# An encoder layer in split-float32 matmuls: a written-out step sequence for every weight block, 121 seven-product pairs for 116, joined weight sums, and q/k/v scaling moved to ScalarE

## The chip, the cores and the metric

The kernel runs on one core of one Trainium2 chip. The metric is the device time of one execution in microseconds (us); the median of the runs counts. The engines are TensorE (PE; its weight loads are listed as PEld), VectorE (DVE), ScalarE (ACT), GpSimd (POOL) and SyncE (SP, which issues the loads).

## The reference, cut to what matters

One encoder layer on 256 tokens of width 4096, all in float32. Nearly all the work is in the large matrix products:

```python
h = rms_norm(x, g_mix[i])
proj = einsum('bsd,de->bse', h, w_in[i])          # 4096 x (1024+512+64 + 5*2048)
c_q, c_kv, k_rope, gate_a, q_b, k_b, v_b, gate_b = split(proj, ...)
... # latent attention (16 heads) from c_q, c_kv, k_rope through w_uq, w_ukv
... # dilated attention (16 heads) from q_b, k_b, v_b
y_a = rms_norm(y_a, g_out_mla[i]) * silu(gate_a)
y_b = rms_norm(y_b, g_out_dil[i]) * silu(gate_b)
x = x + einsum('bse,ed->bsd', concatenate([y_a, y_b]), w_out[i])      # 4096 x 4096
ple = einsum('bsc,cd->bsd', p[i], w_ple[i])
gate = sigmoid(einsum('bsd,de->bse', rms_norm(x, g_ple[i]), w_ple_gate[i]))  # 4096 x 4096
x = x + ple * gate
return rms_norm(x, g_final)
```

## The kernel before, in words

**One product is three matmuls.** Float32 operands are split in two parts, `hi` (a rounded copy, made by ScalarE) and `lo` (the rest, made by VectorE as `src - hi`); `mm` adds hi x hi, hi x lo and lo x hi into one bank of PSUM. So each 512 KB row block of weights that arrives in a buffer `raw` costs a conversion: 1024 columns on ScalarE and 1024 on VectorE.

**Blocks.** The large products are cut into 18 blocks of 1024 weight columns (`Block`): six for the dilated q, k and v (called D0 to D5 here), five for the latent query and the gates (G0 to G4), three for `w_out` (O0 to O2) and four for `w_ple_gate` (P0 to P3). Each block goes over 32 rows of 128 weights (k-rows), with two token tiles A1 and A2 and two column halves of 512, so that there are four results. A block has two kinds of steps:

- A *plain* step (`plain_step`, `c` in an order string) takes one k-row: four products, 12 matmuls.
- A *fast pair* (`fast_steps`, four `f` in an order string) takes two k-rows at once by the seven products of Strassen's method in Winograd's form. Its four steps issue M1; M2 and M3; M5 and M7; M6 and M4: seven products, 21 matmuls, where two plain steps have 24. For them VectorE makes four sums of weights (512 columns each), which are then split into hi and lo as well. The sums of activations that a pair needs are made once for all the blocks that share them (`add_sums`: `x_sums` for D, `x_sums2` for G, `y_sums` for O, `x1_sums` for P).

The seven products add up in eight banks: M1, M5, M6 and M7 belong to the fast pairs, M2, X, M3 and M4 to both kinds. After the last fast step of a block a task called *mid* (`d_mid`, `gate_mid`, `out_mid`, `wide_mid`) combines M1, M5, M6 and M7 in SBUF, while the block's trailing plain steps run; the next block's M2, X, M3 and M4 use the banks that mid reads. After the last step a task *done* adds the other four banks. In the D blocks and in G0 mid and done also multiply each token by its normalisation factor `rx`, as the scalar operand of VectorE's instructions.

**The order of steps.** `spread(n, lead, trail)` makes a block's sequence from three numbers: a lead of plain steps, n pairs and the rest of the plain steps mixed by a fixed cost balance, and a trail of plain steps. `FAST_QKV`, `FAST_G`, `FAST_O` and `FAST_P` give the pairs of each block: 3 7 8 8 8 7, 3 6 7 7 7, 6 7 6 and 7 7 7 5, 116 in all.

**The order of the work around them.** Every engine runs its instructions in the order in which the program issues them. The program keeps a planning clock (`Clock`) with a cost for each instruction, converts the weights a few steps ahead of PE (`convert`, `lead` is `AHEAD` = 2 steps, and 3 more where a block has further places for converted weights), and runs the tasks (mid, done, sums, transposes, attention heads) in the gaps that this clock sees (`advance`). Loads are issued by SP into four `raw` buffers in turn; a pair needs two of them at once.

**Gates and heads.** An attention head's output is copied from PSUM by ScalarE (`attend`), later multiplied by the gate and by the gain of the branch's norm in `gate_rest`, one head (256 columns) at a time.

Of the kernel before, what the change touches and what calls it, by code (L numbers as in the profile page):

```python
# [12 lines left out]
F32 = mybir.dt.float32  # L13
# [21 lines left out]
WARM = 6, 3  # L35

# [174 lines left out]
def encoder_layer(ctx: ExitStack, tc: tile.TileContext, x, p, positions, g_mix, w_in, g_q_latent, w_uq,  # L211
# [30 lines left out]
    def plain(t):  # L242
        return t.bitcast(F32)

# [344 lines left out]
    def attend(h, q_src, k_src, pe, v, y, dil):  # L589
# [96 lines left out]
        nc.scalar.activation(y, by_token(o) if dil else o, AF.Copy)  # L686
# [16 lines left out]
    def head_unit(name, load, product, tags, done, n=2, time=48 * 0.119):  # L703
# [3 lines left out]
        def step(j):  # L707
            box = []

            def get():  # L710
                box.append(clock.made(wp.tile([P, 2, Q], F32, tag="raw", name=f"raw_{name}_{j}", bufs=RAW), "raw", RAW))
                load(box[0], j)
# [11 lines left out]
            new.ring, new.ring_id = HEADS_RING, "heads"  # L724
# [104 lines left out]
    def turn_steps(n, tags):  # L829
# [4 lines left out]
        def step(j):  # L834
            box = []

            def load():
                box.append(clock.made(wp.tile([P, 2, Q], F32, tag="raw", name=f"raw_r{n}_{j}", bufs=RAW), "raw", RAW))
# [19 lines left out]
            new.ring, new.ring_id = HEADS_RING, "heads"  # L858
# [53 lines left out]
    def gate_rest(dil, c, u):  # L912
# [6 lines left out]
        for b in range(2):  # L919
# [17 lines left out]
    QUARTERS = (0, 0, "M2"), (1, 1, "X"), (0, 1, "M3"), (1, 0, "M4")  # L937

    def gate_mid(tags, blk, after=()):

        def task():
# [9 lines left out]
            for d, a, b in (((1, 1), (0, 0), "M6"), ((1, 0), (1, 1), "M5"), ((0, 1), (1, 1), "M7"),  # L951
                            ((1, 1), (0, 1), "M5")):
                nc.vector.tensor_tensor(e[d[0]][:, d[1]], e[a[0]][:, a[1]], ps[b], op=ALU.add)
# [58 lines left out]
    def d_mid(key, blk):  # L1012
        def task():
# [11 lines left out]
            yield from awaited("rx")  # L1025
            sc = [(rxq if key[0] == "q" else rx)[:, t:t + 1] for t in range(NT)]

            def add(h, t, m, old):
                nc.vector.scalar_tensor_tensor(d[h][:, t], ps[m], sc[t], old, op0=ALU.mult, op1=ALU.add)
# [12 lines left out]
    def d_done(key, blk):  # L1042
        def task():
# [3 lines left out]
            for m, t, h in quarters[2:] + quarters[:2] if key == ("v", 1) else quarters:  # L1047
                nc.vector.scalar_tensor_tensor(d[h][:, t], blk.ps[m], sc[t], d[h][:, t], op0=ALU.mult, op1=ALU.add)
# [88 lines left out]
    class Step:  # L1137

        banks, holds, ahead = (), (), False
# [4 lines left out]
        def __init__(self, load, split, run, needs=(), frees=0, time=2.73):  # L1144
            self.load, self.split, self.run, self.needs, self.frees, self.after = load, split, run, needs, frees, None
            self.hold, self.mid = 0, False
# [5 lines left out]
    class Block:  # L1152
# [19 lines left out]
        def step(self, which, *args):  # L1172
            new = Step(*args)
            new.n = self.q
# [12 lines left out]
        def load(self, kt):  # L1187
            kt = self.row(kt)
            r = clock.made(wp.tile([P, 2, self.q], F32, tag="raw", name=f"raw_{kt}", bufs=RAW), "raw", RAW)
# [4 lines left out]
        def plain_step(self, kt):  # L1194
            box, first_ = [], self.late and kt == 16
# [17 lines left out]
            return [self.step("M2 X M3 M4", lambda: box.append(self.load(kt)), both, run, self.needs(kt), 1)]  # L1213

        def fast_steps(self, j):

            r, T = [], []
# [4 lines left out]
            def sub(dst, a, b):  # L1222
                nc.vector.tensor_tensor(dst, a, b, op=ALU.subtract)

            def split1(hi, lo):
                if isinstance(self.tmp, tuple):
                    T.extend(slot(b, [2, self.q]) for b in self.tmp)
                else:
                    both = slot(self.tmp, [4, self.q])
                    T.extend((both[:, :2], both[:, 2:]))  # L1230
                sub(T[0][:, 0], r[0][:, 1], r[0][:, 0])
                sub(T[0][:, 1], r[0][:, 1], r[1][:, 1])
                split(hi[:, 0], lo[:, 0], r[0][:, 0])

            def split2(hi, lo):
                nc.scalar.activation(hi, r[1], AF.Copy)
                sub(T[1][:, 0], r[1][:, 1], T[0][:, 0])
                sub(T[1][:, 1], r[1][:, 0], T[1][:, 0])
                nc.vector.tensor_tensor(lo, r[1], plain(hi), op=ALU.subtract)

            def run(*which):
                def go(hi, lo):
                    for i, (m, a) in enumerate(which):
# [5 lines left out]
            return [  # L1249
                self.step("M1", tuple(lambda k=k: r.append(self.load(k)) for k in (2 * j, 2 * j + 1)), split1, run(("M1", A11)), needs, 1, 0.69),  # L1250
                self.step("M2 M3", None, split2, run(("M2", A12), ("M3", S(3))), needs, 1, 1.37),
                self.step("M5 M7", None, lambda hi, lo: split(hi, lo, T[0]), run(("M5", S(0)), ("M7", S(2))), more, 0, 1.37),
                self.step("M6 M4", None, lambda hi, lo: split(hi, lo, T[1]), run(("M6", S(1)), ("M4", A22)), more, 0, 1.37),
            ]

    def add_sums(n, pair, dst, tmp, name, out, free=lambda j: True, first=0):
# [3 lines left out]
        def task():  # L1260
# [10 lines left out]
            for j in range(first, n):  # L1271
# [806 lines left out]
```

## Time and profile before

| what | value |
|---|---|
| runs of the kernel | 1898.52, 1899.08, 1900.08 us |
| median | 1899.08 us |
| profiled execution, span from first to last instruction | 1897.4 us |
| the same beside the median of the runs | 1.7 us less (its own device time is not listed apart) |
| busy: PE / PEld / DVE / ACT | 1878.5 / 1579.8 / 1696.8 / 1140.2 us |
| weights and other loads | 364.72 MB read, 194 GB/s over the span |

The busy time of an engine is the union of its instructions' durations. The durations of matmuls overlap, so that the time from the start of one to the start of the next is the measure, and a busy PE can still have small gaps; a stretch without gaps is seen in the sum of the weight loads, since each matmul has one of about the same length. An instruction's row has its start, its duration, the engine, the kernel's line (here always that of a helper), the operation, what it writes and reads by the program's names, and its shape.

### The profile page before, as it was taken

Reading aid. Unit: us, or ns where it says so; the run is one execution under the profiler, and the core shown is the slowest. Engines: PE = TensorE matmul, PEld = TensorE weight load, DVE = VectorE, ACT = ScalarE, POOL = GpSimd, SP = SyncE. Lnnn points to the kernel's source line nnn. Section 1 sums busy time; section 2 is a strip of 40 time slices with the busy share of each in tenths; the row PEclk is TensorE's granted clock in tenths of the full one; section 3 lists DMA queues with packets and bytes.
Section 4 is the critical chain, followed back from the end, with each engine's and each line's share of the span. In section 5 each row is a group of like instructions: output and inputs, shape, how many; then the busy total and the mean of one; then the engine's idle time right before and its main releaser. Section 6 shows DMA issues by size and latency. Waiting matters only on the chain.

```text
span 1897.4 us, 25417 instructions
## 1 busy us (share of the span) xinstructions
PE 1878.5 (99%) x9133; PEld 1579.8 (83%) x9133; DVE 1696.8 (89%) x2354; ACT 1140.2 (60%) x1543; POOL 31.2 (2%) x41
## 2 busy tenths in 40 slices
PE   9999999999999999999999999999999999999997
PEld 7888888888899888888888999888888888888885
DVE  6999999899898989999998777999989989989897
ACT  7655656565588555556556556656655555666654
POOL 0000000000011000000000010100000000000000
PEclk9999999999999999999999999999999999999999
DMA  8666666666735566666667553576666666665665
GB/s 279 189 205 213 214 212 200 198 213 193 218 84 159 166 211 183 196 215 189 208 199 209 137 142 123 167 231 204 216 199 217 187 194 218 194 223 183 221 222 180
DMA packets 160871, 370.59 MB, mean 195 GB/s; under 512 B 29116, under 2 KB 70952, under 8 KB 160744
## 3 DMA queue, kind: packets, MB, share of 16 engines
q1 hardware_dynamic: 159896, 366.58, 62.0%
q0 software_dynamic: 512, 1.84, 0.3%
q8 instruction: 72, 1.18, 0.3%
q10 hardware_dynamic: 336, 0.54, 0.1%
q14 instruction: 55, 0.45, 0.1%
HBM read 364.72 MB, written 4.19 MB: 194 GB/s over the span
## 4 chain that ended last, share of the span: by engine, by line
PE 85%; DVE 10%; DMA 2%; issue 2%; ACT 1%; POOL 0%; DVEq 0%; ACTq 0%; POOLq 0%
PE m L177 49%; PE t L177 16%; PE s L177 11%; PE o L177 9%; DVE lo L177 3%; DVE B L177 3%; DVE T L177 2%; DVE Ah L177 1%; DMA raw<-in_w_ple_gate_dram 1%; DVE Al L177 1%; DMA raw<-in_w_in_dram 1%; ACT hi L177 0%; DVE st L177 0%; ACT B L177 0%; DVE B7b L177 0%
## 5 line engine op out<-in xcount | busy, mean ns | idle before, releaser
L177 ACT ACTIVATE hi<-raw 128x1024 fp32r<-128x1024 f32 (+2 forms) x396 | 378.9, 966 | 278.1 <-PE m L177 70.9
L177 DVE TENSOR_TENSOR lo<-raw,hi 128x1024 fp32r<-128x1024 f32 (+2 forms) x396 | 433.4, 1107 | 61.8 <-ACT hi L177 60.6
L177 PE MATMUL m<-hi,Ah 128*128 128x512 f32 (+2 forms) x659 | 247.2, 387 | 0.3 <-ACT hi L177 0.3
L177 DVE TENSOR_TENSOR B<-raw,B 128x1024 fp32r<-128x1024 f32 (+3 forms) x228 | 213.9, 947 | 20.5 <-ACT B L177 18.8
L177 PE MATMUL m<-hi,Al 128*128 128x512 f32 (+2 forms) x625 | 229.6, 380 | 0.0
L177 PE MATMUL m<-lo,Ah 128*128 128x512 f32 (+2 forms) x549 | 207.8, 379 | 1.4 <-DVE lo L177 1.3
L177 ACT ACTIVATE B<-raw 128x1024 fp32r<-128x1024 f32 (+2 forms) x142 | 135.3, 962 | 96.8 <-DMA raw<-in_w_in_dram 25.3
L177 PE MATMUL m<-hi,B 128*128 128x512 f32 (+1 forms) x524 | 179.0, 389 | 0.0
L177 PE MATMUL m<-B,Ah 128*128 128x512 f32 (+2 forms) x554 | 146.7, 359 | 0.6 <-DVE B7b L177 0.6
L177 PEld LDWEIGHTS m<-hi,Ah 128*128 128x128 f32 x659 | 124.0, 188 | 22.7 <-ACT hi L177 1.2
L177 PEld LDWEIGHTS m<-hi,Al 128*128 128x128 f32 x625 | 117.5, 188 | 21.8
L177 PEld LDWEIGHTS m<-lo,Ah 128*128 128x128 f32 x549 | 103.4, 188 | 19.9 <-DVE lo L177 2.9
L177 PEld LDWEIGHTS m<-hi,B 128*128 128x128 f32 x524 | 98.2, 188 | 19.6
L177 PEld LDWEIGHTS m<-B,Ah 128*128 128x128 f32 x554 | 95.9, 189 | 15.3 <-DVE B7b L177 1.0
L177 PE MATMUL m<-lo,B 128*128 128x512 f32 (+1 forms) x262 | 102.1, 390 | 0.1
L177 PE MATMUL m<-B,Al 128*128 128x512 f32 (+2 forms) x289 | 99.1, 371 | 0.0
L177 DVE TENSOR_TENSOR T<-raw,T 128x512 f32<-128x512 f32 (+2 forms) x110 | 85.5, 789 | 3.3 <-ACT T L177 1.7
L177 ACT ACTIVATE hi<-B 128x1024 fp32r<-128x1024 f32 x57 | 59.4, 1056 | 23.1 <-PE m L177 7.3
L177 DVE TENSOR_TENSOR lo<-B,hi 128x1024 fp32r<-128x1024 f32 x57 | 68.5, 1220 | 3.9 <-ACT hi L177 3.6
L177 PE MATMUL t<-hi,Ah 128*128 128x512 f32 x184 | 69.9, 391 | 0.0
L177 ACT ACTIVATE B<-T 128x1024 fp32r<-128x1024 f32 (+2 forms) x55 | 50.2, 916 | 22.8 <-DVE T L177 13.4
L177 PEld LDWEIGHTS m<-B,Al 128*128 128x128 f32 x289 | 54.4, 188 | 9.2
(530 smaller groups left out, 4336.9 us busy)
## 6 DMA issues: line engine op xcount, KB each, us to landing
raw<-in_w_in_dram SPq DMA_DIRECT2D x359, 512.0 KB, 4.3
raw<-in_w_out_dram SPq DMA_DIRECT2D x128, 512.0 KB, 4.6
raw<-in_w_ple_gate_dram SPq DMA_DIRECT2D x128, 512.0 KB, 4.7
raw_q<-in_w_uq_dram SPq DMA_DIRECT2D x32, 256.0 KB, 3.8
T<-in_x_dram SPq DMA_DIRECT2D x13, 512.0 KB, 6.6
raw<-in_w_in_dram SPq DMA_DIRECT2D x16, 320.0 KB, 3.1
raw_r<-in_w_uq_dram SPq DMA_DIRECT2D x16, 256.0 KB, 4.3
raw_k<-in_w_ukv_dram SPq DMA_DIRECT2D x16, 256.0 KB, 3.4
```

The lines of the kernel that those rows point to most:

```text
L177: return do(out, *rest, **named)
```

## The change

Every block gets its own sequence, written out as a string (`c` plain step, `f` quarter of a fast pair, `e` a step of the per-layer embedding), instead of `spread`. The numbers of pairs become 2 8 8 8 8 8 for D, 3 6 8 8 8 for G, 6 7 7 for O and 7 7 7 5 for P: 121. `x_sums2` and `x1_sums` make eight sets of sums instead of seven, and sets that had a place of their own now go into columns of the activations that fast pairs no longer read (`odd`).

The signs of the weight sums are turned (sums instead of differences, and the two products M5 and M7 change places), so that the first two can be made by one instruction on 2 x 512 columns, whose first operand is repeated and whose second has a stride; for that the four `raw` buffers become slots of one tile, and a pair takes two adjacent ones where it can. Where they aren't adjacent, two instructions are issued as before. `add_sums` joins two of its operations in the same way.

In the D blocks and G0, mid and done no longer multiply by `rx`. After done, four copies of 512 columns in place do it, on ScalarE unless the planning clock has VectorE free earlier by 0.3. The branch's gain is applied when ScalarE copies the head's output, and `gate_rest` multiplies two heads in one instruction.

```diff
+ORDER_D = (
+    "cccccccccccccccccccfcffccfccfcfffccc",
+    "ccccfcffffcffcffcfffccffcfcfffffcffffffffcffffcc",
+    "cccccffffffffcfccfcfcfcfffffcfffffcffffffcffffcc",
+    "cccfcfcffcffffcffcffcfffcccffffffffffcfcffffffcc",
+    "ccfffcffcccfffcffffffffcfccfffcfcfffcffffffcffcc",
+    "ccfccfcffcffffffffcfffffcffffcffcfffccfffffccfcc",
+)
+ORDER_G = (
+    "cccccccccccccccfccfffcfffcfcfcfcccffcc",
+    "cccfcccccfffcccfffcffffffcffcfffffcffffccccc",
+    "cccccfcccfffffcfffffffcfffcfffffcfcffffffcffffcc",
+    "cccccfcfccffffffffcffcffffffffcffffffcffcffffccc",
+    "ccfcfffccfcffffccffffffffcffcfffffccffffcffffccc",
+)
+ORDER_O = (
+    "ccfccfcccffffcfffccfcffcfffcccfffffffcffcccc",
+    "cccfcfcccffffcffffffcffcffcfffcfcfffcfffffcccc",
+    "ccccffccfffcffffcffcffcfffcffcfffffcffffcfcccc",
+)
+ORDER_P = (
+    "ccccfcfccffffffcffcfffcfcfcfffcfffcffffcfffccce",
+    "ccffcccffcffffccffffffcfccffffcffffffcfccffccec",
+    "cccfcfffccccfffffcffcffcffcffffffffcffccfffccce",
+    "ccccfffcfcfcfcfffffcfccffffffffccc",
+)
...
+    RAW = 4
+    raw_all = wp.tile([P, 2 * RAW, 512], F32, tag="raw", name="raw_all", bufs=1)
+    raw_free = list(range(RAW))
...
-        nc.scalar.activation(y, by_token(o) if dil else o, AF.Copy)
+        nc.scalar.activation(y, by_token(o) if dil else o, AF.Copy, scale=G["ob" if dil else "oa"][:, h:h + 1])
...
-            for k in range(2):
-                h = 4 * c + 2 * b + k
-                g = G["ob" if dil else "oa"][:, h:h + 1]
-                y = yb_rows(h) if dil else by_token(y_rows(ya, h))
-                nc.vector.scalar_tensor_tensor(y, y, g, by_token(tp[:, k]), op0=ALU.mult, op1=ALU.mult)
...
+            nc.vector.tensor_tensor(y, y, u_, op=ALU.mult)
...
+    def mix(e, ps):
+        nc.vector.tensor_tensor(e(1, 1), e(0, 0), ps["M6"], op=ALU.add)
+        nc.vector.tensor_tensor(e(1, 0), ps["M5"], e(1, 1), op=ALU.subtract)
+        nc.vector.tensor_tensor(e(0, 1), e(1, 1), ps["M7"], op=ALU.subtract)
+        nc.vector.tensor_tensor(e(1, 1), ps["M5"], e(0, 1), op=ALU.subtract)
...
-            for t in range(NT):
-                nc.scalar.activation(d[0][:, t], ps["M1"], AF.Copy, scale=sc[t])
-            for t in range(NT):
-                add(1, t, "M6", d[0][:, t])
-            add(0, 1, "M7", d[1][:, 1])
-            add(1, 0, "M5", d[1][:, 0])
-            add(1, 1, "M5", d[0][:, 1])
+            nc.scalar.activation(d[0][:, 0], ps["M1"], AF.Copy)
+            mix(lambda h, t: d[h][:, t], ps)
...
-                nc.vector.scalar_tensor_tensor(d[h][:, t], blk.ps[m], sc[t], d[h][:, t], op0=ALU.mult, op1=ALU.add)
+                nc.vector.tensor_tensor(d[h][:, t], blk.ps[m], d[h][:, t], op=ALU.add)
+            yield from awaited("rx")
+            for m, t, h in quarters[2:] + quarters[:2] if key == ("v", 1) else quarters:
+                if clock.free["dve"] + 0.3 < clock.free["act"]:
+                    nc.vector.tensor_scalar(d[h][:, t], d[h][:, t], sc[t], None, op0=ALU.mult)
+                else:
+                    nc.scalar.activation(d[h][:, t], d[h][:, t], AF.Copy, scale=sc[t])
...
-                sub(T[0][:, 0], r[0][:, 1], r[0][:, 0])
-                sub(T[0][:, 1], r[0][:, 1], r[1][:, 1])
+                at = slots[0][0]
+                if slots[1][0] == at + 1:
+                    plus(T[0], raw_all[:, 2 * at + 1:2 * at + 2].to_broadcast([P, 2, self.q]),
+                        raw_all[:, 2 * at:2 * at + 4:3])
+                else:
+                    plus(T[0][:, 0], r[0][:, 1], r[0][:, 0])
+                    plus(T[0][:, 1], r[0][:, 1], r[1][:, 1])
...
-                two(ALU.add, u[:, 0], a[:, 1], a[:, 3])
-                two(ALU.subtract, u[:, 1], u[:, 0], a[:, 0])
-                two(ALU.subtract, u[:, 2], a[:, 1], a[:, 0])
-                two(ALU.subtract, u[:, 3], a[:, 2], u[:, 1])
+                two(ALU.subtract, u[:, 0:3:2], a[:, 1:2].to_broadcast([P, 2, P]), a[:, 0:4:3])
+                two(ALU.subtract, u[:, 1], u[:, 2], a[:, 0])
+                two(ALU.add, u[:, 3], a[:, 2], u[:, 1])
...
-    FAST, WIDE, LAST_K = 7, 4, 8
-    FAST_P, LEAD_P, TRAIL_P = (7, 7, 7, 5), (6, 6, 6, 4), (4, 4, 4, 4)
+    FAST, WIDE, LAST_K = 8, 4, 8
...
-    PLACES = "B5", "Ah2", "Al2", "B0", None, None, None, ""
+    PLACES = "B5", "Ah2", "Al2", "B0", None, None, None, "Ah3"
...
-    FAST_QKV, LEAD_QKV = (3, 7, 8, 8, 8, 7), (18, 4, 4, 4, 4, 4)
-    FAST_G, LEAD_G = (3, 6, 7, 7, 7), (15, 10, 6, 6, 4)
-    FAST_O, LEAD_O = (6, 7, 6), (4, 5, 4)
...
-        order = spread(FAST_QKV[n], LEAD_QKV[n], (3, 2, 2, 2, 2, 5)[n])
+        order = ORDER_D[n]
```

More of the change, by code (lines that the diff above doesn't have):

```diff
@@ L1194, in plain_step, with get @@
         def plain_step(self, kt):
-            box, first_ = [], self.late and kt == 16
+            box, slots, first_ = [], [], self.late and kt == 16
+            def get():
+                slots.extend(raw_slots())
+                box.append(self.load(kt, slots))
             def run(hi, lo):
@@ L1211, in both @@
                     split(hi, lo, box[0])
-            return [self.step("M2 X M3 M4", lambda: box.append(self.load(kt)), both, run, self.needs(kt), 1)]
+            new = self.step("M2 X M3 M4", get, both, run, self.needs(kt), 1)
+            new.slots = slots
+            return [new]
         def fast_steps(self, j):
-            r, T = [], []
+            r, T, slots = [], [], ([], [])
             (A11, A21), (A12, A22) = [[lambda k=k, t=t: tuple(q[:, t * P:(t + 1) * P] for q in self.lhs(k))
@@ L1517, in both @@
                 END["kept"].append((hi, lo))
-            new = Step(lambda: box.append(blk.load(kt)), both, lambda hi, lo: part(0, j), [], 1, 0.69 * (1 + (j >= SKEW)))
+            new = Step(get, both, lambda hi, lo: part(0, j), [], 1, 0.69 * (1 + (j >= SKEW)))
+            new.slots = slots
             new.halves = lambda: place(j)
```

178 lines of the change are left out of this document (93 added, 85 removed).

## The prediction

> **What bounds the kernel now.** I read the page's busy shares and chain first, then the chain in order of time, then busy time by stretch, then single instructions.
>
> ```profile
> span 1897.4 us, 25417 instructions
> ...
> PE 1878.5 (99%) x9133; PEld 1579.8 (83%) x9133; DVE 1696.8 (89%) x2354; ACT 1140.2 (60%) x1543; POOL 31.2 (2%) x41
> ...
> PE 85%; DVE 10%; DMA 2%; issue 2%; ACT 1%; POOL 0%; DVEq 0%; ACTq 0%; POOLq 0%
> ```
>
> ```profile
> 347.35 10.88 PE m L177 x48
> ```
>
> TensorE (PE) fills the span and the chain. In the second fence 48 matmuls of 512 columns take 10.88 us: 0.2267 us each, with no gap. So this kernel gets faster by fewer matmuls or fewer gaps. How many gaps there are is seen from the weight loads (PEld, the second busy column), one for each matmul:
>
> ```profile
> 50.00:100.00 50.00, 49.72 (x223) 40.76 (x222) 48.77 (x92) 30.72 (x42) 0.00 (x0) 1.00 0.63 195
> 100.00:150.00 50.00, 49.96 (x221) 40.87 (x220) 49.59 (x69) 29.00 (x35) 0.00 (x0) 1.00 0.64 200
> 150.00:200.00 50.00, 49.39 (x218) 40.60 (x217) 47.62 (x59) 26.02 (x30) 0.00 (x0) 1.00 0.69 216
> 1400.00:1450.00 50.00, 49.71 (x224) 40.32 (x223) 42.06 (x52) 28.64 (x38) 0.00 (x0) 1.00 0.68 216
> 1800.00:1850.00 50.00, 49.69 (x220) 40.82 (x219) 48.86 (x63) 29.94 (x37) 0.00 (x0) 1.00 0.69 221
> 1650.00:1700.00 50.00, 50.00 (x223) 41.39 (x222) 47.47 (x53) 30.30 (x32) 0.00 (x0) 1.00 0.68 223
> ```
>
> The last row is a full stretch (41.39). The deficits of the others, scaled by 50/41.39, are 0.8, 0.6, 1.0, 1.3 and 0.7 us: 4.3 us of gaps where steps of the two kinds alternate. VectorE (DVE, third column) is at 49.59 of 50 in one of them: it is the next limit, and the change adds work to it and takes work from it.
>
> **1. Five more pairs.** A plain k-row is 4 products, a pair of k-rows by seven products is 7 instead of 8, and a product is 3 matmuls. 121 pairs for 116 save 5 x 3 = 15 matmuls: 15 x 0.2267 = 3.40 us. Nothing covers that, since PE is the chain.
>
> **2. What a pair costs VectorE.** Pitches, from start to start, in a stretch with no idle time:
>
> ```profile
> 302.92 0.68 DVE L177 TENSOR_TENSOR T<-raw 128x512 f32<-128x512 f32 x1
> 303.52 0.68 DVE L177 TENSOR_TENSOR T<-raw,raw 128x512 f32<-128x512 f32 x1
> 304.12 0.68 DVE L177 TENSOR_TENSOR B<-raw,B 128x512 fp32r<-128x512 f32 x1
> 304.72 1.41 DVE L177 TENSOR_TENSOR T<-raw,T 128x512 f32<-128x512 f32 x2
> 306.05 2.36 DVE L177 TENSOR_TENSOR B<-raw,B 128x1024 fp32r<-128x1024 f32 x2
> 308.32 1.22 DVE L177 TENSOR_TENSOR lo<-T,hi 128x1024 fp32r<-128x1024 f32 x1
> ```
>
> 512 columns take 0.60 us (302.92 to 303.52), 1024 take 1.135 (306.05 to 308.32, two). A pair now has four 512-wide sums, one 512-wide and three 1024-wide subtractions: 5 x 0.60 + 3 x 1.135 = 6.40 us. Two plain rows have 2.27. With the first two sums made in one instruction (1.135 for 1.20) it is 6.33; where the two weight buffers don't lie side by side it stays 6.40, and if the repeated operand read costs more than a plain one, the gain is lost. I take 6.33. Five pairs: 5 x (6.33 - 2.27) = +20.3 us; the other 116: -8 (0 to -8).
>
> **3. q/k/v scaling.** In the block ends the scale rode on nine VectorE instructions. Here is one such middle on DVE, and PE beside it:
>
> ```profile
> 180.98 1.40 DVE L177 SCALAR_TENSOR_TENSOR B7b<-m,st,B7a 128x512 f32<-128x512 f32 x2
> 182.41 0.75 DVE L177 SCALAR_TENSOR_TENSOR B7a<-m,st,B7b 128x512 f32<-128x512 f32 x1
> 183.08 0.74 DVE L177 SCALAR_TENSOR_TENSOR B7b<-m,st,B7b 128x512 f32<-128x512 f32 x1
> 183.74 0.74 DVE L177 SCALAR_TENSOR_TENSOR B7b<-m,st,B7a 128x512 f32<-128x512 f32 x1
> 184.40 1.22 DVE L177 TENSOR_TENSOR lo<-raw,hi 128x1024 fp32r<-128x1024 f32 x1
> ```
> ```profile
> 183.53 0.39 PE L177 MATMUL m<-B,Al 128*128 128x512 f32 x1
> 184.54 0.50 PE L177 MATMUL m<-B,Ah 128*128 128x512 f32 x1 [0.61 <-DVE B7b L177]
> ```
>
> The five take 180.98 to 184.40 = 3.42 us. PE should go on at 183.53 + 0.23 = 183.76 and does so at 184.54: its next product writes the bank that the last of the five reads. With four plain instructions at 0.60 the middle ends 2.40 us after 180.98, at 183.38, before PE asks. That gap of 0.77 us goes; what is late next there is the conversion of part 6. Over seven such blocks (six q/k/v, one latent) VectorE has 9 x 0.667 - 8 x 0.60 = 1.2 us less each, -8.4 in all.
>
> ```profile
> L177 ACT ACTIVATE B<-B,st 128x512 f32<-128x512 f32 x20 | 13.5, 708 | 0.0
> L177 DVE TENSOR_SCALAR T<-T,st 128x256 f32<-128x256 f32 x32 | 10.2, 362 | 0.6
> L177 DVE SCALAR_TENSOR_TENSOR B<-B,gT,t 128x256 f32<-128x256 f32 x8 | 3.5, 475 | 0.0
> L177 DVE TENSOR_TENSOR B<-B 128x128 f32<-128x128 f32 x60 | 14.8, 288 | 1.0
> ```
>
> ScalarE (ACT) gains four scaled copies a block at 13.5/20 = 0.68 us and loses one of two in the middle: +2.0 us a block, +14 in all, on an engine idle 40% of the time. I cost it at nothing, covered by that idle time and by the converted weights that stand ready; rival C is that cover gone.
>
> **4. Smaller edits.** The gate product takes one 512-wide instruction for two 256-wide: two at about 0.475 - 0.08 (what a 512-wide one's 0.68 overlaps its 0.60 pitch) = 0.80 for 0.60, x16: -3.2 us of DVE. Activation sums: two 128-wide operations in one, about -0.07 x 29 = -2.0; but two more sets are made (an eighth for the gates, an eighth that the last phase doesn't use): each 2 x 0.60 + 0.33 + 2 x 0.21 = about 1.95, +3.9. The head output's gain rides on 32 copies that ScalarE makes anyway; each costs between nothing and a whole scaled copy (0.68), and I take it near nothing, as no element more is written. All of it is off PE; gain or loss on the path 0, bounds -0.5 to +1.
>
> DVE in total: +20.3 - 8.1 - 8.4 - 3.2 - 2.0 + 3.9 = +2.5 us on 1696.8. Its share stays 89 to 90%. So the question isn't the sum but which block gets it.
>
> **5. Weights' loads.** The same bytes in the same order; the four buffers become slots of one tile with a pair taking two at once, as two had to be free before. Taken as 0.
>
> **6. Where the pairs go.** Windows over blocks (D1, D2, D3 of q/k/v, gates G2, G3, G4, output block O2; my bounds, within a step):
>
> ```profile
> 101.70:184.00 82.30, 82.18 (x362) 67.36 (x360) 79.54 (x106) 47.13 (x56) 0.00 (x0) 1.00 0.67 208
> 184.00:265.60 81.60, 81.06 (x358) 67.12 (x359) 79.34 (x93) 46.39 (x51) 0.00 (x0) 1.00 0.66 210
> 265.60:347.20 81.60, 81.60 (x362) 67.57 (x361) 76.36 (x89) 47.67 (x50) 0.00 (x0) 1.00 0.64 206
> 770.00:854.00 84.00, 84.00 (x380) 69.56 (x379) 78.30 (x96) 50.09 (x56) 0.00 (x0) 1.00 0.66 204
> 854.00:938.00 84.00, 84.00 (x380) 69.60 (x379) 77.75 (x94) 50.30 (x56) 0.00 (x0) 1.00 0.66 200
> 938.00:1022.00 84.00, 84.00 (x373) 69.54 (x372) 74.95 (x86) 47.44 (x51) 0.00 (x0) 1.00 0.67 197
> 1403.00:1487.00 84.00, 83.71 (x375) 68.46 (x374) 73.81 (x91) 48.34 (x61) 0.72 (x1) 1.00 0.67 215
> ```
>
> D2 and D3 have eight pairs already, and run at 97% and 94% of DVE with no gap but the 0.77. G2, G3, G4, O2 and D1 get one more each. G3: 77.75 + 4.06 - 7 x 0.07 - 0.8 (gate products) = 80.5 of 83.3 (84 less 0.68): 97%. G4 93%; O2 77.4 of 83.3, 93%. G2 also has the added sums: 83.0 of 83.3, full. D1: 79.54 + 4.06 - 0.5 - 1.2 - 0.3 = 81.6 of 81.6, full, unless the activation sums made in it move to block D0, which loses a pair (4.06 us of room). The lone plain rows that the new sequences put at G1's end and G2's start (five each, 2.72 us of PE for 1.135 of DVE) leave 10 x 1.6 = 16 us for those sums, so I take both as fitting: cost 0, bounds 0 and rival B.
>
> **The sum.** 1899.08 - 3.40 - 0.77 = **1894.9 us**. It is a difference from the median of the runs, 1899.08; the profiled execution's span is 1897.4, 1.7 us under it, and its shares are used as they are. 0.2% of it, 3.8 us, is about what a measurement of this kernel can tell: the matmuls alone (3.40) fall just short, with the gap (4.17) just past it.
>
> **Rivals.** *A2, the other gaps close too* (better placed sequences): up to the 4.3 us above, 1899.08 - 3.40 - 4.3 = 1891.4. For it: the gaps lie where VectorE is fullest. Against: those at 1400 have DVE at 42 of 50, so there it is order, not load.
>
> *B, VectorE fills up where a pair was added.* D2 shows that 97% is carried. Beyond that G2 lacks 83.0 - 0.97 x 83.3 = 2.2 us and D1 81.6 - 0.97 x 81.6 = 2.4: 1894.9 + 2.2 = 1897.1 with one, 1899.5 with both: no change. For it: the two full blocks. Against: room in D0 and in the plain rows.
>
> *C, the scaling blocks ScalarE's queue: slower.* The four copies wait for four VectorE additions that wait for the block's last products; behind them on ACT stand the next weights' conversions, for which VectorE and then PE wait. Price: 4 x 0.60 + 4 x 0.68 = 5.1 us without a conversion. What stands ready at that place, just after the middle shown above:
>
> ```profile
> 190.51 1.82 DVE L177 TENSOR_TENSOR lo<-raw,hi 128x512 fp32r<-128x512 f32 x2
> ```
> ```profile
> 195.55 0.39 PE L177 MATMUL m<-hi,Ah 128*128 128x512 f32 x1
> ```
>
> The second of these two ends at 192.33 and is used at 195.55: 3.2 us ahead. 5.1 - 3.2 = 1.9 us for each of seven blocks: 1894.9 + 13.3 = 1908.2. It decides from 4.17 + 3.8 = 8.0 us, 1.1 us a block. Against: after the change the middle takes 1.0 us less, so the reserve is larger; and the code gives a copy to DVE when ACT is behind in its plan. The Trainium skill, page "ScalarE: Activation LUTs", Rules for kernel authors, speaks for this rival: multiplications belong on VectorE rather than ScalarE. By that rule the move costs; the trace shows VectorE's 256-wide scaling at 0.362 us against ScalarE's 0.68 for 512, thus no clear loss per element, and ScalarE with the idle time.
>
> *D, one tile for all weight buffers* makes each load wait until all earlier ones are read:
>
> ```profile
> raw<-in_w_in_dram SPq DMA_DIRECT2D x359, 512.0 KB, 4.3
> ```
>
> 4.3 us from issue to landing, where PE needs a row every 2.72: 359 x 1.6 = 570 us more, 2465. Against it: the new slots are addressed apart.
>
> **How the numbers follow.** The forecast 0.38 and A2 0.12 make faster 0.50 (1891.4 to 1895.3); the matmuls alone, with the gap kept or another for it (1895.7), 0.12 and B 0.26 make no change 0.38 (1895.3 to 1902.9); C 0.10 and D 0.02 make slower 0.12. Likeliest 1894.9, its own range 1893 to 1896; the range 1891 to 1899.5 takes in A2 and both blocks of B, and leaves out C, D and the little that goes beyond either end.
>
> **What would show it.** 15 matmuls fewer; no gap above 0.5 us at the start of the third q/k/v block; DVE busy 1695 to 1703; ACT busy 1155 to 1170; weight loads back at a full stretch's 41.4 in the first 200 us. It is wrong if PE waits on DVE in G2 or D1 (B), or if ACT idles on DVE's sums at block ends with PE gaps 3 to 6 us later (C).

## The result: slower, and the profile after

The changed kernel takes 1931.88 us (median of 5, 1926.96 to 1934.55) against 1898.6 for the kernel before in the same runs: ratio 1.0167, 95% interval 1.0153 to 1.0181. The forecast was 1894.9, with a range up to 1899.5.

The page of the changed kernel, with its span, its busy time by engine and its chain of waits:

```profile
span 1930.1 us, 25264 instructions
...
PE 1889.3 (98%) x9118; PEld 1576.1 (82%) x9118; DVE 1704.3 (88%) x2234; ACT 1165.3 (60%) x1579; POOL 30.8 (2%) x41
...
PE 60%; DVE 23%; DMA 10%; issue 3%; ACT 3%; DVEq 0%; SPq 0%; ACTq 0%
```

Work is nearly as forecast: 15 matmuls fewer (9133 to 9118), DVE 1704 us, ACT 1165 us. The chain is not. PE's share fell from 85% to 60%; DVE has 23% instead of 10%, and DMA 10% instead of 2%. No engine became full, so the loss is waiting. What PE waits for, first in the changed kernel, then the row of the same name before (columns: us in total, times, longest):

```profile
PE m L204 <- DVE lo L204: 13.6, 20, 1.5
PE m L204 <- DVE B L204: 3.3, 8, 0.7
PE s L204 <- DVE B L204: 2.7, 3, 1.5
```
```profile
PE m L177 <- DVE lo L177: 1.3, 3, 0.8
```

All gaps between matmuls, counted in the traces as the time from start to start less the pitch of the matmul's width (0.2267 us for 512 columns), sum to 17.7 us before and 54.5 after: +36.8. (The first expectation below has 16.7 and 48.9 from an earlier count.) Less 15 x 0.2267 = 3.4 that is +33.4, the whole of the 33.3 us by which the medians differ. This count takes in matmuls that ran at half pace, some 3 us of it (last section). The windows of the prediction's part 6, now of the changed kernel (span of the window, busy PE, PEld, DVE, ACT, POOL, clock, DMA share, GB/s):

```profile
101.70:184.00 82.30, 81.09 (x356) 66.37 (x355) 79.36 (x92) 48.31 (x55) 0.00 (x0) 1.00 0.65 207
184.00:265.60 81.60, 81.60 (x362) 67.59 (x361) 77.99 (x85) 49.60 (x55) 0.00 (x0) 1.00 0.67 212
265.60:347.20 81.60, 81.60 (x362) 67.59 (x361) 75.80 (x81) 49.84 (x54) 0.00 (x0) 1.00 0.64 199
770.00:854.00 84.00, 83.98 (x377) 68.97 (x377) 80.26 (x90) 52.14 (x59) 0.00 (x0) 1.00 0.63 195
854.00:938.00 84.00, 82.33 (x368) 66.92 (x367) 80.56 (x89) 51.66 (x57) 0.00 (x0) 1.00 0.64 198
938.00:1022.00 84.00, 83.02 (x363) 67.36 (x362) 76.98 (x85) 48.46 (x53) 0.00 (x0) 1.00 0.62 197
1403.00:1487.00 84.00, 78.91 (x339) 62.51 (x339) 71.06 (x81) 47.45 (x60) 0.00 (x0) 0.98 0.60 193
```

The largest loss, in the last row, is where VectorE is least busy (71.06 of 84). An engine that idles while PE waits for it is itself waiting. For what, the groups of instructions say; these are the pairs' first two sums made in one instruction (busy time, mean ns | idle time before them and what ended it):

```profile
L204 DVE TENSOR_TENSOR T<-raw_all 128x1024 f32<-128x1024 f32 x38 | 46.4, 1221 | 11.2 <-DMA raw_all<-in_w_in_dram 10.8 <-DVE lo L204 0.4
L204 DVE TENSOR_TENSOR Ah<-raw_all 128x1024 f32<-128x1024 f32 x22 | 26.9, 1224 | 17.9 <-DMA raw_all<-in_w_ple_gate_dram 15.5 <-issue 2.2
L204 DVE TENSOR_TENSOR Al<-raw_all 128x1024 f32<-128x1024 f32 x7 | 8.6, 1222 | 6.0 <-DMA raw_all<-in_w_out_dram 5.9
```

In the kernel before, the first of the pair's two sums hardly waits, whichever tile it writes:

```profile
L177 DVE TENSOR_TENSOR T<-raw 128x512 f32<-128x512 f32 x41 | 28.0, 683 | 0.0
L177 DVE TENSOR_TENSOR Ah<-raw 128x512 f32<-128x512 f32 x26 | 18.0, 691 | 1.1 <-DMA raw<-in_w_ple_gate_dram 0.4
```

So VectorE now waits for weights. The chain in the stretch 1455 to 1486 us (block O2) shows the circle (start, us, what ended last):

```profile
1461.54 5.41 DMA raw_all<-in_w_out_dram
1466.95 0.03 issue
1466.98 0.05 DVEq L204
1467.03 0.04 issue
1467.07 1.23 DVE Al L204
1468.30 0.60 DVE lo L204
1468.90 0.61 DVE Al L204
1469.51 0.02 issue
1469.54 0.04 DVE Al L204
1469.57 0.57 issue
1470.14 1.23 DVE lo L204
1471.38 0.02 issue
1471.39 5.84 DMA raw_all<-in_w_out_dram
```

Read it as a ring: a load starts at 1461.54 and lands 5.41 us later; VectorE makes the joined sum, M1's `lo`, the other sums, and at 1470.14 the `lo` that reads the second row. That frees the pair's buffers, and 0.02 us later the next load of this ring starts, at 1471.39. PE isn't in it. One turn takes 9.85 us, for two k-rows of the pair and one plain row of 4.76 + 2.72 = 7.5 us of PE's time (21 and 12 matmuls by 0.2267). So buffers come round too late, though the loads themselves are hardly slower: the median from issue to landing is 3.9 us for `w_in` (4.3 before), 4.7 for `w_out` (4.6) and 4.8 for `w_ple_gate` (4.7).

Which slot each of these loads goes into can be read off the kernel's program, whose loads and conversions come in the same order as the trace's. All pairs of this stretch use slots 0 and 1. The load that starts at 1461.54 goes into slot 1, free since 1461.52, while slot 3 had been free since 1456.03; the one at 1471.39 goes into slot 1 again, while slot 2 had been free since 1462.65. Each time the free slot is filled only by the plain row's load that is issued next, 0.4 us later.

### The profile page after: what moved, and what is told of

Its sections match the earlier page's. It is cut to its first block, busy times and chain, and to the rows that moved or that the text cites. A ratio compares the mean times of both kernels' runs of the same rounds, so it can differ in the third digit from the quotient of the medians.

```text
span 1930.1 us, 25264 instructions
## 1 busy us (share of the span) xinstructions
PE 1889.3 (98%) x9118; PEld 1576.1 (82%) x9118; DVE 1704.3 (88%) x2234; ACT 1165.3 (60%) x1579; POOL 30.8 (2%) x41
## 4 chain that ended last, share of the span: by engine, by line
PE 60%; DVE 23%; DMA 10%; issue 3%; ACT 3%; DVEq 0%; SPq 0%; ACTq 0%
PE m L204 36%; PE t L204 11%; DVE lo L204 8%; PE s L204 7%; DVE B L204 6%; PE o L204 6%; DMA raw_all<-in_w_in_dram 4%; DMA raw_all<-in_w_ple_gate_dram 4%; DVE T L204 3%; DVE Ah L204 3%; DMA raw_all<-in_w_out_dram 2%; DVE Al L204 1%; ACT hi L204 1%; DVE B7b L204 1%; ACT B L204 1%
## 5 line engine op out<-in xcount | busy, mean ns | idle before, releaser
L204 ACT ACTIVATE hi<-raw_all 128x1024 fp32r<-128x1024 f32 (+2 forms) x432 | 416.4, 973 | 290.1 <-DMA raw_all<-in_w_in_dram 69.3
L204 DVE TENSOR_TENSOR lo<-raw_all,hi 128x1024 fp32r<-128x1024 f32 (+2 forms) x432 | 478.8, 1119 | 73.1 <-ACT hi L204 71.2
L204 PE MATMUL m<-hi,Ah 128*128 128x512 f32 (+2 forms) x642 | 240.7, 388 | 0.9 <-ACT hi L204 0.9
L204 DVE TENSOR_TENSOR B<-raw_all,B 128x1024 fp32r<-128x1024 f32 (+3 forms) x232 | 217.2, 942 | 16.6 <-ACT B L204 14.3
L204 PE MATMUL m<-lo,Ah 128*128 128x512 f32 (+2 forms) x536 | 203.5, 380 | 4.6 <-DVE lo L204 4.6
L204 ACT ACTIVATE B<-raw_all 128x1024 fp32r<-128x1024 f32 (+2 forms) x140 | 134.6, 967 | 107.6 <-DMA raw_all<-in_w_in_dram 40.6
L204 PE MATMUL m<-hi,B 128*128 128x512 f32 (+1 forms) x534 | 183.9, 391 | 0.3 <-DVE B L204 0.3
L204 DVE TENSOR_TENSOR T<-raw_all,T 128x512 f32<-128x512 f32 (+2 forms) x113 | 87.5, 787 | 1.6
L204 PEld LDWEIGHTS m<-lo,B 128*128 128x128 f32 x267 | 50.4, 189 | 19.6 <-DVE lo L204 10.3
```

The source lines that it names most:

```text
L204: return do(out, *rest, **named)
```

## The experiments

Two theories were open: *slots* (the choice of two neighbouring buffers makes loads wait) and *sequences* (the written-out orders of steps load VectorE in bursts); a third was rival C, the scaling on ScalarE. Differences in us below are between medians. Stage times are of one profiled execution each: q/k/v blocks, gates, heads with output blocks, last phase, and the tail after the last matmul, cut at the first matmul of the next stage.

**Slots by age.** The changed kernel's pair looks for two neighbouring free slots; here it takes the two that have been free longest.

```
-        if n == 2:
-            got = next(([a, a + 1] for a in raw_free if a + 1 in raw_free), got)
```

> The changed kernel, but a pair takes the two weight slots that have been free longest instead of two adjacent ones; where they happen to be adjacent the first two sums are still joined, else they are two instructions (DVE +0.07 us each). The changed kernel has 48.9 us of gaps between matmuls by my count of its trace, against 16.7 before, and in them VectorE's first sum waits for a load. Theory T1 (slots): the pair's first load waits for the younger slot while the older lies free, so that two loads start at once and late; then most of the 32 us goes: 1895 to 1905 us. Theory T2 (sequences): runs of fast steps ask for loads faster than four buffers can bring them, whichever slot is taken: 1920 to 1933. Theory T3 (scaling blocks ScalarE's queue): unchanged, 1927 to 1935.

1907.61 us, ratio 1.0045 [1.0028, 1.0061]: 24.3 us of the loss gone, a quarter left. DMA's share of the chain falls from 10% to 4%, and

```profile
PE m L204 <- DVE lo L204: 3.3, 7, 0.8
```

instead of 13.6. What the slots do was counted over 472 loads of the traces (from the end of the last conversion that read a slot to the issue of the next load into it). In the changed kernel a slot lies free 0.53 us on average, 252 us in all, 53 times over 1 us; by age 0.04 us, 17 us, twice. Then 4.3 us to land and 6.0 to 6.4 held: about 10.9 us a turn in four slots, a k-row each 2.7 us, the pace of PE (2.72 for a plain row, 2.38 for one of a pair). That the two agree doesn't show by itself that there is no reserve, since a landed row is also held while it waits its turn: by a count of the same kind over the 505 or 506 loads that can be paired, 2.6 us of the time held pass before the first read in the changed kernel, 3.0 in the kernel before (where a slot lies free 0.03 us). The reserve is missing at single loads: 29% of them are read within 0.15 us of landing in the changed kernel, 20% by age, 19% before. SP issues in order: a load put on a younger slot while the older lies free holds up every load behind it, as in O2 above.

**The old sequences** in the changed kernel (116 pairs), with its neighbouring slots and by age.

```
-ORDER_D = (...), ORDER_G, ORDER_O, ORDER_P      # written out, 121 pairs
+ORDER_D = (...), ORDER_G, ORDER_O, ORDER_P      # as spread() made them before, 116 pairs
```

> The changed kernel with the sequences of before (116 pairs, lead and trail as before), all else as changed: adjacent slots, joined sums, scaling on ScalarE. T1: adjacency delays loads here too, but the old sequences put at most a few fast steps in a row: 1902 to 1915. T2: the waits are gone with the sequences: 1896 to 1900. T3: 1925 to 1935, since the scaling is still on ScalarE.

> Old sequences (116 pairs) and the slots that have been free longest; joined sums where they happen to fit, scaling on ScalarE. T1 and T2: 1895 to 1900, and the difference to the old sequences with adjacent slots is what adjacency costs there (T1: 4 to 15 us, T2: under 2). T3: 1920 or more.

1936.91 us (1.0195 [1.018, 1.021]) and 1901.64 (1.0014 [1.0004, 1.0023]). So the written-out sequences aren't the main cost: without them, and with neighbouring slots, the kernel is slower still. (How much slower says little: the two profiled spans differ by 2.6 us, and the old sequences have 27 matmuls at half pace where the changed kernel has 14, at 0.2 us each; see the last section.) By age they are worth -6.0 us when taken out, though their five pairs should save 3.4.

**Which part of the slot choice.** The older of the two neighbours is loaded first; and neighbours are kept but the joined sum made as two instructions.

```
+   late = n == 2 and raw_free.index(got[0]) > raw_free.index(got[1])
+   made = {k: self.load(k, own) for k, own in (both[::-1] if late else both)}
```
```
-                if slots[1][0] == at + 1:
+                if False:
```

> The changed kernel with adjacent slots and joined sums, but of a pair's two loads the one into the slot that was freed earlier is issued first. T1: the early load starts when its slot is free, and half or more of the 32 us goes: 1896 to 1915 (less than with the slots by age, because a pair must still find two neighbours). T2 and T3: 1925 to 1935.

> The changed kernel (adjacent slots, new sequences), but the first two weight sums are always two instructions. Slots by age took the changed kernel from 1931.9 to 1907.6 us, and did two things at once: other slots, and 23 joined sums for 109. Theory S (the choice of slots) says that this kernel stays slow, 1922 to 1935. Theory J (the joined instruction: it can start only when both rows are there, and the first row's slot is released 0.5 us later) says 1904 to 1912.

1925.64 us (1.0137 [1.0122, 1.0152]) and 1918.51 (1.0107 [1.0087, 1.0126]), the second between what the two theories expected. The issue order within the pair is a small part (6.2 us; slots still lie free 215 us in all), since slots that are older than both are passed over too. With two sums the slots lie free just as long (245 us over 506 loads, 250 in the changed kernel by the same count), yet 13.4 us are gone. The joined sum adds them where loads are late: VectorE, in order, stands at it until both rows are there, where two instructions could work on the first.

**Joined without neighbours**: one instruction for slots a and b, read at the stride between them.

```
+   at = raw_all[:, 2 * a_:2 * b_ + 2:2 * (b_ - a_) + 1] if a_ < b_ else ...
+   plus(T[0], raw_all[:, 2 * a_ + 1:2 * a_ + 2].to_broadcast([P, 2, self.q]), at)
```

> New sequences, slots by age, and the first two sums always joined, with the stride that the two slots give (the two results change places where the first slot is the higher one). S: as with the slots by age, 1904 to 1910. J: back up to 1920 to 1932.

1906.58 us, 1.0038 [1.0023, 1.0053]: the same as two instructions by age (1907.61). So the joined sum isn't what costs, and needs no neighbours. VectorE's busy time falls by 5.9 us (1708.6 to 1702.7), the time by nothing that can be told.

**Two suspects that did nothing**: the q/k/v scaling back on VectorE, and M1's `lo` ahead of the pair's second sum (both by age; in the second run the sums are always two instructions).

```
-   nc.vector.tensor_tensor(d[h][:, t], blk.ps[m], d[h][:, t], op=ALU.add)   # and a scaled ScalarE copy
+   nc.vector.scalar_tensor_tensor(d[h][:, t], blk.ps[m], sc[t], d[h][:, t], op0=ALU.mult, op1=ALU.add)
```
```
     plus(T[0][:, 0], r[0][:, 1], r[0][:, 0])
+    split(hi[:, 0], lo[:, 0], r[0][:, 0])
     plus(T[0][:, 1], r[0][:, 1], r[1][:, 1])
-    split(hi[:, 0], lo[:, 0], r[0][:, 0])
```

> New sequences, slots by age, and q/k/v scaled by VectorE's instructions as before the change (nine scaled instructions a block for eight plain ones and four copies on ScalarE). If the scaling on ScalarE blocks conversions (T3) this is faster than 1907.6 by 3 us or more: under 1904. If VectorE is what is short, it is slower: 1909 to 1915, with gaps in the first 500 us. If neither: 1905 to 1909.

> New sequences, slots by age, two sums always, and VectorE's subtraction for M1, which needs the first row alone, before the sum that needs the second: once the second row has landed, the first slot is free 0.6 us sooner. If the time from a slot's load to its release (its turnaround, with four slots) is what limits, the gaps shrink: 1898 to 1905 against 1907.6. If it isn't: 1906 to 1909.

1907.66 us (1.0042 [1.0027, 1.0057]) and 1907.4 (1.0043 [1.0029, 1.0057]), against 1907.61. Rival C has no price here; nor has the move a gain with these sequences, though it takes 9.9 us off VectorE (1718.5 to 1708.6).

**What is left of the sequences.** By age and joined, the gaps of gate block G3 have a plain look. VectorE's rows of the first sums of three pairs in a row (the stretch 896 to 918 us, in which VectorE never idles), and PE in it:

```profile
899.21 1.22 DVE L204 TENSOR_TENSOR B<-raw_all 128x1024 f32<-128x1024 f32 x1
...
906.83 1.22 DVE L204 TENSOR_TENSOR B<-raw_all 128x1024 f32<-128x1024 f32 x1
...
913.41 1.23 DVE L204 TENSOR_TENSOR B<-raw_all 128x1024 f32<-128x1024 f32 x1
```
```profile
915.87 0.40 PE L204 MATMUL s<-hi,Ah 128*128 128x512 f32 x1
917.76 0.51 PE L204 MATMUL s<-lo,Ah 128*128 128x512 f32 x1 [1.49 <-DVE lo L204]
```

A pair costs VectorE 7.62 and 6.58 us here (other work lies in the first), PE 4.76. Two pairs without a plain row between them put VectorE some 4.7 us behind, and PE then waits 917.76 - 915.87 - 0.23 = 1.66 us. Three runs asked whether the length of such runs of `f` is the whole story. All three are by age and joined, and have the last phase's old sequences: all other blocks evenly spread at 121 pairs; the written-out sequences in D, G0 to G2 and O, with the old ones in G3 and G4 (119 pairs; here gates 3 and 4 read columns that an eighth set of sums has overwritten, so part of the gates is computed from other data, and only the time counts); and the same but for G3 and G4 evenly spread at eight pairs.

```
-ORDER_G = (..., "cccccfcfccffffffffcffcffffffffcffffffcffcffffccc", ...)
+ORDER_G = (..., "ccccfcfcfffcffffcffffcfcffffcfffcffffcffffcfffcc", ...)    # G3, G4 evenly spread
```

> Slots by age, sums always joined, the new counts of pairs (121), but each block's sequence made by the evenly spreading rule of before, with the old leads and trails. The written-out sequences with slots by age stand at 1906.6 us, the old ones with 116 pairs at 1901.6. If the rest of the loss is the written-out order (long runs of fast steps where a reserve is small: gates 3 and 4, the start and end of the last phase), this gives 1896 to 1900. If it is the number of pairs (VectorE full), the gaps in the gates stay and it gives 1902 to 1907.

> Slots by age, sums always joined; written-out sequences for q/k/v, the latent query, gates 1 and 2 and the output blocks, the old ones (7 and 7 pairs) for gates 3 and 4 and for the last phase: 119 pairs. By the trace of the kernel with slots by age the two replaced parts hold 3.4 and about 5 us of gaps more than before. If gaps stay where they were seen, 1896 to 1899 (2.0 us of matmuls and about 1 us of gaps less than before, 1.5 us of gaps more in the output blocks). If gaps only move, 1901 or more.

> Slots by age, sums joined, 121 pairs, written-out sequences but for gates 3 and 4, which get the evenly spread sequence of a q/k/v block (eight pairs, no more than four fast steps in a row, two plain steps at the end), and for the last phase, which gets its old ones. The written-out ones run eight fast steps in a row there, and the trace shows VectorE without idle time through such a run while PE waits. If the runs are the cause: the gaps of 900 to 1000 us and of the last phase go, 1898 to 1901. If VectorE is short in these blocks with eight pairs however they are laid: 1902 to 1906.

1911.01 us (1.0061 [1.0047, 1.0074]), 1899.71 (1.0003 [0.9994, 1.0012]) and 1908.12 (1.0047 [1.0035, 1.006]); the first and the last lie above all that was expected of them. With even sequences the gap at 900 to 950 us is there all the same (3.73 us by the count of gaps), with 4.18 at 800 to 850. Where only G3 and G4 are even, those of 900 to 1000 are gone (3.2 us to nothing), but 2.83 us stands at 850 to 900 and 5.41 at 1050 to 1100. So the runs theory is half right: it names the mechanism of the gap at 916 us, but even sequences at eight pairs don't remove the cost. The last two of these runs differ in G3 and G4 alone: the eighth pair of each costs 8.4 us there. Where the gaps then stand it isn't a run of `f` that makes them: the one at 873 us ends with ScalarE, and at 1051 us, among the heads, PE waits 2.8 us for VectorE and then runs at half pace. Why two more pairs end there wasn't traced. With 119 pairs, and without the new sequences of the last phase (354.8 us there to 350.7), the time is that of before, with nine matmuls fewer.

In the last phase, too, most of the 4.1 us is no run of `f`. In the kernel by age and joined, 3.4 us of gaps lie at 1866 to 1872, and the chain there is a load:

```profile
1860.45 8.22 DMA raw_all<-in_w_ple_dram
...
1868.78 1.06 ACT hi L204
...
1869.87 1.24 DVE lo L204
...
1871.15 0.96 PE m L204 x3
```

VectorE idles 2.55 us just before that `lo`. What makes this load take 8.22 us from issue to landing (4.4 is the median of its kind before) wasn't tested.

**The kernel before with the written-out q/k/v sequences alone.**

```
-        order = spread(FAST_QKV[n], LEAD_QKV[n], (3, 2, 2, 2, 2, 5)[n])
+        order = ORDER_D[n]
```

> The kernel before, with the written-out sequences for the six q/k/v blocks alone (42 pairs for 41); its four buffers in turn, its sums and its scaling on VectorE stay. In the trace of the changed kernel with slots by age this stage ended 1.5 us earlier than before (one pair, 0.68, and gaps). If that stage's gain stands by itself: 1896.5 to 1898.5 beside about 1899. If it needs the lighter VectorE work of the change, gaps come back in the first 250 us: 1899 to 1902.

1900.33 us, 1.0006 [0.9997, 1.0015]; q/k/v stage 511.4 for 511.1. In the changed kernel by age and joined the same sequences give 509.7, 1.4 us less than before, as much as the forecast's 0.68 for one pair more in these blocks and 0.77 for the gap together; that it is these two wasn't shown. What they need beside themselves wasn't isolated: the scaling on ScalarE it is not, since the run by age with the scaling on VectorE has 509.9.

**The residue with old sequences** (1901.64): seven sets of activation sums, or the gain again in the gate's instruction.

```
-    FAST, WIDE, LAST_K = 8, 4, 8
+    FAST, WIDE, LAST_K = 7, 4, 8
```
```
-        nc.scalar.activation(y, by_token(o) if dil else o, AF.Copy, scale=G["ob" if dil else "oa"][:, h:h + 1])
+        nc.scalar.activation(y, by_token(o) if dil else o, AF.Copy)
...
+                nc.vector.scalar_tensor_tensor(y, y, g, by_token(tp[:, k]), op0=ALU.mult, op1=ALU.mult)
```

> Old sequences, slots by age (1901.6 us), without the eighth set of sums that the last phase doesn't use. If that set holds the last transposed input back (1.3 us of gaps after 1550 us more than before): 1899.5 to 1900.8. If not: 1901 to 1902.5.

> Old sequences, slots by age (1901.6 us), but the branch's gain again multiplied with the gate, one head per instruction, and not in ScalarE's copy of the head's output. If the gain on ScalarE, in the stretch of the heads where it is fullest, costs: 1899 to 1901. If the joined gate product helps: 1902 to 1904. If neither: 1901 to 1902.5.

1901.35 us (1.0015): no effect of the sums. 1898.79 (1.0002 [0.9993, 1.0011]) with the gain in the gate, which also makes the gate's product one head at a time again: 2.9 us less by the medians, 2.3 by the ratios, 1.5 between the two profiled runs, where the stage of the heads goes from 513.1 to 510.6 us. ScalarE's group of head copies, first with the scale, then without (mean ns after the comma):

```profile
L204 ACT ACTIVATE B<-o,gT 128x256 f32<-128x256 f32 x16 | 7.4, 464 | 3.4 <-PE o L204 3.4
```
```profile
L204 ACT ACTIVATE B<-o 128x256 f32<-128x256 f32 x16 | 6.0, 372 | 3.5 <-PE o L204 3.4
```

0.09 us a copy, 32 x 0.09 = 3 us of ScalarE. The intervals of the two kernels overlap from 1.0004 to 1.0011, so this is likely rather than shown, and how ScalarE's 3 us reach the path wasn't traced.

**Putting together what paid**: by age, joined, the q/k/v sequences alone (117 pairs; the first expectation says 116), gain in the gate; then the same with two first sums.

```
+ORDER_D = (written out); ORDER_G, ORDER_O, ORDER_P = (as before)
+nc.vector.scalar_tensor_tensor(y, y, g, by_token(tp[:, k]), op0=ALU.mult, op1=ALU.mult)
```
```
-                plus(T[0], raw_all[:, 2 * a_ + 1:2 * a_ + 2].to_broadcast([P, 2, self.q]), at)
+                plus(T[0][:, 0], r[0][:, 1], r[0][:, 0])
+                plus(T[0][:, 1], r[0][:, 1], r[1][:, 1])
```

> A version put together from what paid: slots by age with the first two sums joined, the scale of q/k/v on ScalarE, the written-out sequences in the q/k/v blocks alone (116 pairs in all), the gain in the gate's instruction as before, seven sets of activation sums. If the costs found so far add up, the stages are those of the runs that had each part: q/k/v 509.6 us (slots by age with own sequences; 511.1 before), gates 511.5, heads and output 510.6, last phase 350.5, tail 12.9: 1895.1 by the trace, 0.9975 to 0.9985 of the kernel before. If stages hand their lateness on (a block that starts earlier only waits longer at the next one), the 1.5 us of the q/k/v blocks is lost again behind them: 1898.5, 1.000. If the joined sum needs its pair's second load so early that it costs where old sequences are used, 1900 to 1903.

> The run before (joined sums, old sequences in gates, output and last phase) with its pairs' first two sums as two instructions. The theory that the joined sum costs where an old sequence lets the pair's second load come late: the gaps at 750 to 800 us (2.67) and 1250 to 1300 us (3.77) go back to those of the run with the gain in the gate and old sequences (0.16 and 1.12); with q/k/v at 509.6, gates 511.9, heads and output 510.6, last phase 351, tail 12.9 the time is 1896 and the ratio 0.9975 to 0.999. The rival, that the q/k/v blocks' new sequences hand a lateness on to the gates and heads whatever the sum's form: the gaps stay and the time is 1902 to 1904.

1903.65 us (1.0027 [1.0018, 1.0036]), and 1900.14 (1.0002 [0.9993, 1.0011]). The first is 6.8 us above the sum (span 1901.9 for 1895.1 by the trace), the second some 4 above the 1896 that was expected. With two sums the gap at 750 to 800 goes from 2.67 us to 0.16 and that at 1250 to 1300 from 3.77 to 1.86, but the q/k/v stage gives back 1.0 (509.5 to 510.5). So the joined sum does cost in some places and pay in others, and terms of 1 to 3 us don't add from one version to the next. No version beat the kernel before; at 1.0002 it is equalled.

## Why the prediction was wrong, by its steps

**Part 5, the loads, "Taken as 0": the step that failed.** It argued from the count of buffers, "as two had to be free before". What counts is which two, and when each fell free: 24.3 us of the 33 go with the two lines that pick neighbours. A sum that could have warned was at hand: 4.3 us from issue to landing against one row every 2.72, with four buffers, leaves 4 x 2.72 - 4.3 = 6.6 us in which a buffer may wait, be read and be freed. In the kernel before, a row lies landed for 3.0 us on average and is then being read for 3.5, and 19% of the rows are read as soon as they land. The changed choice makes single loads wait for a slot far longer than that reserve: in O2 slot 2 lay free for 9.1 us. And a sum that reads both rows at once starts with the later one. Rival D asked about the same tile, but only whether slots share a wait, not in which order they are taken. The forecast had nothing on it.

**Parts 1 to 3: right as counts.** 15 matmuls went. The joined sum costs 1.22 us where two cost 1.29, as taken; the gap at 183.76 closed (with the scaling on VectorE and the new sequences it is 0.32 us, so less than half of the 0.77 belongs to the scaling). ScalarE has the 28 scaled copies more, four for each of seven blocks; this group has 24 of them, 44 for 20:

```profile
L204 ACT ACTIVATE B<-B,st 128x512 f32<-128x512 f32 x44 | 28.9, 710 | 2.1 <-DVE B L204 2.0
```

DVE 1704.3 lies 1 us past the forecast's 1695 to 1703, ACT 1165.3 within 1155 to 1170. In the first 200 us the weight loads came back to a full stretch in the first two windows only:

```profile
50.00:100.00 50.00, 50.00 (x226) 41.37 (x225) 47.37 (x91) 30.43 (x42) 0.00 (x0) 1.00 0.67 195
100.00:150.00 50.00, 50.00 (x222) 41.28 (x221) 48.36 (x59) 29.91 (x38) 0.00 (x0) 1.00 0.64 205
150.00:200.00 50.00, 48.79 (x214) 39.72 (x214) 48.63 (x54) 31.32 (x35) 0.00 (x0) 1.00 0.61 193
```

The third row is D1's second half, named as full in part 6: 1.8 us of gaps.

**Part 4, the head's gain "near nothing": too low.** It measured 0.09 us a copy, between the ends given (0 and 0.68). The run without it gains 1.5 to 2.9 us where +1 was the bound; that this is the copy's cost is likely, not shown. The estimate looked at the copy alone, not at what stands behind it.

**Part 6 and rival B: the mechanism seen, partly in another place.** With the slots mended (by age and joined), PE does wait on a full VectorE, most in G3 (2.33 and 0.83 us at 900 to 1000, where B gave 2.2 to a block). Of the blocks that B named, D1 has 1.2 us of gaps, 0.95 of them at 165 us, where VectorE has had no idle time for 10 us; before, nearly all of D1's gaps were the 0.77 at its end. G2 has 0.4 us. The last phase cost most (354.8 for 350.7), and there most of it is a late load, not a full VectorE. In G3 averages over a block hid it: G3 was put at 97% of VectorE and D2 shows that 97% can be carried; a run of two pairs is not an average.

**Rivals C and D**: C had no price (1907.66 with the scaling on VectorE, 1907.61 on ScalarE). The rule of the Trainium skill, page "ScalarE: Activation LUTs", Rules for kernel authors, that multiplications belong on VectorE, makes no difference here: 1.0042 and 1.0045 (the page gives its reason for bf16; the data here are float32). D's ring of all loads didn't come.

## What to carry to other kernels

Before a change to buffers is costed at nothing, look at how long a landed buffer waits for its first read, load by load (over a steady stretch the average turn agrees with the pace of the bound engine whatever the reserve); where many loads have no such reserve, the order in which buffers are reused is as important as their count, and the oldest free one is to be loaded first. An in-order engine that needs two transfers in one instruction turns the later of them into its own start. Small terms from single edits were not additive here: order them by measurement, not by sum.

## What was not expected of the hardware

After bunched gaps the matmuls run at half pace for 3.41 us. In the changed kernel, PE at 1479 to 1486 us (start, us):

```profile
1479.58 0.63 PE L204 MATMUL m<-hi,Ah 128*128 128x512 f32 x2
1481.71 0.50 PE L204 MATMUL m<-lo,Ah 128*128 128x512 f32 x1 [1.50 <-DVE lo L204]
1482.05 0.40 PE L204 MATMUL m<-hi,Ah 128*128 128x512 f32 x1
...
1482.92 0.63 PE L204 MATMUL s<-hi,Al 128*128 128x512 f32 x1
1483.35 1.49 PE L204 MATMUL m<-B,Al 128*128 128x512 f32 x3
1484.63 1.47 PE L204 MATMUL t<-B,Ah 128*128 128x512 f32 x3
```

From 1482.92 on a matmul takes 0.43 us (three in 1.28) instead of 0.2267, and again at 1623 to 1626. The granted clock (the third number from the end, 1.00 and then 0.50) shows it, here for the stretch before and the stretch itself:

```profile
1479.12:1482.53 3.41, 1.79 (x7) 1.16 (x8) 3.38 (x5) 3.41 (x4) 0.00 (x0) 1.00 0.52 153
1482.53:1485.94 3.41, 3.41 (x10) 2.67 (x9) 3.41 (x4) 1.17 (x2) 0.00 (x0) 0.50 0.70 196
```

Eight matmuls and then six by 0.2 us: some 3 us of the loss are not the gaps themselves but what follows them. The Trainium skill, page "TensorE: Matmul & The Clock Gate", section "What's actually happening", has the clock halved after an idle window of about 3.4 us. The pitch and the granted clock agree with a halved clock; but no gap in this trace was longer than 1.68 us (1481.71 - 1479.58 - 2 x 0.2267), so several shorter gaps together are enough. The gaps of the 3.41 us before each of the two spells add up to 2.0 and 2.3 us. The traces of four other runs have six more spells, of 3.41 us or twice that (three with the old sequences and neighbouring slots, one with short runs, one each in the two suspects' runs), and before each the same sum is 2.1 to 3.1 us. Taken in steps of 3.41 us in the phase of the clock's changes, no stretch of any trace with less than 2.0 us of gaps was followed by half pace, and one with 2.1 (neighbouring slots, two sums) was not either.
